# Summing the head outputs' squares where the outputs become final, and an output stage with batched factors, one mixing product, the norm's affine on VectorE and another order of pools

## The chip, the cores and the metric

One core of a Trainium2 chip runs the whole kernel. The metric is the device time of one execution in microseconds (us). The engines are named as in the profile: PE is TensorE (matrix multiplications and transposes; PEld its weight loads), DVE is VectorE, ACT is ScalarE, POOL is GpSimd, SP is SyncE, which issues all transfers between the memory (HBM) and the on-chip memory (SBUF). Matrix products accumulate in PSUM.

## The reference

A trunk of two layers runs over 2048 latent tokens with 256 context tokens in front, model width 1024. All is float32. In each layer the stream is normalised and modulated, projected, and split among three branches: a bidirectional gated delta scan (4 heads of 128 outputs, here A), a neighbourhood attention (4 heads of 64, B) and a bidirectional gated linear attention (4 heads of 64, C, "GLA"). A and C are sums of a forward and a backward pass, and each head of them is divided by its root mean square. Then all are gated, joined and projected, and the result is added to the stream and normalised again:

```
def head_rmsnorm_gate(o, w, z):
    o = o * lax.rsqrt(jnp.mean(o * o, -1, keepdims=True) + 1e-6) * w
    return o.reshape(b_, l, h * dv) * jax.nn.silu(z)
...
    y = concatenate([head_rmsnorm_gate(oa, gdn_norm[i], a_z), ob * silu(b_z),
                     head_rmsnorm_gate(oc, gla_norm[i], c_z)]) @ w_out[i]
    x = layer_norm(DN_ALPHA * x + gate * y) * ln_g[i] + ln_b[i]
```

Layer 0 gives 18 tiles of 128 tokens (2 context, 16 latent), layer 1 the 16 latent ones.

## The kernel before

Each layer of the kernel is a sequence of stages. Every large product is made of three float32 matmuls per 128 rows of depth (high by high, low by high, high by low; `dense_mm`, L185 to L190), so a value that goes into one is first split into a high part (written by ScalarE) and the rest (by VectorE).

The branches leave their outputs in memory. GLA (`Gla.chunk`, `Gla.reverse`) writes its forward output to OC; the reversal reads it back, adds its own part (L558) and stores it again. The delta scan (`Gdn.step`, L978 to L1041) goes forward and backward at once, two heads at a time. A step multiplies on TensorE (pk, pv), scales the result on ScalarE (v, L1013), multiplies again (pd) and updates the state on VectorE; v is on the chain from one step to the next. The direction that reaches a chunk second loads the first one's output from OA (L1035), adds its own (L1036) and stores the sum (L1040). Attention (`Natten.pair`) runs interleaved with the scan.

The output stage is class `Out`. `weights` loads w_out (raw), scales and splits it (wh on ScalarE, L1297; wl on VectorE, L1298). `run` has two parts for each tile. `mixed(n)` loads oa, ob, oc and the gates g, squares and sums each head of oa and oc on ScalarE (L1337, L1338; each writes a sum that a second short instruction reads out), makes the factor r of each head on VectorE with a square root on ScalarE (L1341 to L1346), multiplies outputs, factors and gates on VectorE (4 of 128 columns, L1350; 4 of 64, L1351; one of 256, L1352), transposes the product on TensorE (L1358) and splits it (mh on ScalarE, L1360; ml on VectorE, L1361). `finish(n)` makes the 48 matmuls of the tile into two PSUM tiles py, gates each (L1373), adds the stream x (L1374), takes the statistics, and normalises:

```
            b = P.tile([128, 1], F32, tag="pnb", name="pnb")
            nc.vector.scalar_tensor_tensor(b, mu, -1.0, r, op0=ALU.mult, op1=ALU.mult)
            eng = nc.vector if n == len(tiles) - 1 else nc.gpsimd
...
                nc.scalar.activation(y[:, s], y[:, s], AF.Identity, bias=b, scale=r)
                eng.tensor_tensor(y[:, s], y[:, s], self.g[:, 0, s], op=ALU.mult)
                eng.tensor_tensor(y[:, s], y[:, s], self.g[:, 1, s], op=ALU.add)
```

In layer 0 it also makes the next layer's normalised, modulated and transposed input M from y (`after`, with TensorE's L153 and ScalarE's L135).

The order of instructions on each engine is not written by hand: a scheduler lays the program's instructions out by its own time model, and buffers are taken from pools (a name, a number of buffers, a side of SBUF). A pool opened over memory that earlier tiles still use makes its first writers wait for those tiles. Instructions of one engine run in that order; a wait holds up what is queued behind it.

Of the kernel before, what the change touches and what calls it, by code (L numbers as in the profile page):

```python
# [160 lines left out]
def stage_p1(e, P, ps, xsrc, modT, M):  # L161

    for b in range(NB):
# [8 lines left out]
        for t in range(TPB):  # L172
            modulate(e, P, ps, xs[t], mu[:, t:t + 1], r[:, t:t + 1], b * TPB + t, modT, M)

# [153 lines left out]
class Gla:  # L328
# [180 lines left out]
    def chunk(self, c, i, A, E, et, V):  # L509
        e, nc, P, ps = self.e, self.e.nc, self.p, self.ps  # L510
        t0 = i * 128
        if c >= self.first:
# [10 lines left out]
            nc.sync.dma_start(self.OC[c], o1)  # L523

# [15 lines left out]
    def reverse(self):  # L540
        e, nc, P, ps = self.e, self.e.nc, self.p, self.ps
        for n, c in enumerate([1, 0] + list(range(NT - 1, 1, -1))):
# [17 lines left out]
            nc.sync.dma_start(self.OC[c], o1)  # L560

# [14 lines left out]
class Gdn:  # L576
# [4 lines left out]
    def __init__(self, e, ctx, conv_w, a_log, dt_bias, first):  # L581
# [19 lines left out]
        self.nW = c.tile(sh, F32, name="nW")  # L601
        self.conv_w = conv_w
# [375 lines left out]
    def step(self, s, d, c, n):  # L978
# [55 lines left out]
        if c in s.seen:  # L1034
            nc.sync.dma_start(ot, self.OA[c, :, h0:h0 + 2])  # L1035
            nc.vector.tensor_tensor(ot, ot, po, op=ALU.add)  # L1036
        else:
            s.seen.add(c)
            nc.scalar.copy(ot, po)
# [226 lines left out]
class Out:  # L1266
# [14 lines left out]
    def __init__(self, e, ctx):  # L1281
# [3 lines left out]
        self.P, W1, self.P1, W2 = (pool(n, b, "right") for n, b in (("op", 2), ("ow", 1), ("oi", 2), ("ox", 1)))  # L1285
# [25 lines left out]

    def load(self, P, n, w, src):
# [4 lines left out]
    def run(self, pss, tiles, G2, OA, na, OC, nq, xsrc, xdst, after):  # L1317

        e, nc = self.e, self.e.nc

        def mixed(n):
            t, P, ps = tiles[n], self.P1, pss[n % 2]
            ld = lambda n, w, src: self.load(P, n, w, src)
            oa = ld("oa", 512, OA[t].rearrange("p h d -> p (h d)"))
            ob = P.tile([128, 256], F32, tag="ob", name="ob")
            if t < 2:
                nc.sync.dma_start(ob, na.OBc[t])
            else:
                for i in range(4):
                    o = 64 * (t % 2) + 32 * (i // 2)  # L1330
                    nc.sync.dma_start(ob[32 * i:32 * i + 32], na.OB[t // 2 - 1, i % 2, o:o + 32])
            oc = ld("oc", 256, OC[t])
            g2 = ld("g2", 1024, G2[t])
            ms = P.tile([128, 8], F32, tag="ms", name="ms")
            sq = P.tile([128, 128], F32, tag="sq", name="sq")
            for h in range(4):
                nc.scalar.activation(sq, oa[:, h * 128:(h + 1) * 128], AF.Square, accum_out=ms[:, h:h + 1])  # L1337
                nc.scalar.activation(sq[:, :64], oc[:, h * 64:(h + 1) * 64], AF.Square, accum_out=ms[:, 4 + h:5 + h])  # L1338
            n_ = nq[:, :, t]
            f = P.tile([128, 8], F32, tag="f", name="f")  # L1340
            nc.vector.scalar_tensor_tensor(f[:, 0:4], n_, 1.0 / 128, n_, op0=ALU.mult, op1=ALU.mult)  # L1341
            nc.vector.memset(f[:, 4:8], 1.0 / 64)
# [194 lines left out]
```

## Time and profile before

| | |
|---|---|
| median of 3 runs | 4004.79 us (3985.05 to 4007.02) |
| profiled execution | 3995.01 us |
| its span | 3992.9 us |
| busy in the span: PE, PEld | 3626.0 us (91%), 3113.1 us (78%) |
| busy in the span: DVE, ACT, POOL | 2521.8 us (63%), 1660.0 us (42%), 810.2 us (20%) |
| mean granted PE clock | 0.913 of full speed |

The trace is of one execution. The span runs from its first to its last recorded instruction. Busy times of different engines overlap, and the shares are means over stages that differ.

### The profile page before, as it was taken

The page shows a single profiled execution, that of the slowest core. Times are in us where ns is not written, and L with a number is a line of the kernel's source. Part 1 is how long each engine was busy: PE and PEld are TensorE (multiplying, and loading weights), DVE is VectorE, ACT ScalarE, POOL GpSimd, SP SyncE. Part 2 cuts the span into 40 slices and gives each one's busy share as a digit, 9 for nine tenths or more (in the row PEclk, how much of TensorE's full clock was granted, in tenths as well). Part 3 has the DMA queues.
Part 4 walks back from the last instruction along what each step waited for, and adds up shares of the span by engine and source line. Part 5 has one row for each costly group of instructions (what it writes and reads, how often), then busy time and mean ns, then how long its engine had stood idle before and what let it go on. Part 6 is the DMA issues. An engine that isn't in the chain of part 4 may idle for free.

```text
span 3992.9 us, 77074 instructions
## 1 busy us (share of the span) xinstructions
PE 3626.0 (91%) x27262; PEld 3113.1 (78%) x27262; DVE 2521.8 (63%) x7471; ACT 1660.0 (42%) x4387; POOL 810.2 (20%) x1182
## 2 busy tenths in 40 slices
PE   7999998899989999897898999999999898989788
PEld 3777787579977888896676778887998788879676
DVE  5465462668975676356875556527798766753587
ACT  4533231335433454446545333213454244545342
POOL 0121111210101332221232211112111132331133
PEclk8988988899999998898898888899999998988899
DMA  9843435876687876666647443268776887775753
GB/s 312 280 147 105 133 112 169 245 232 201 205 276 219 246 229 189 187 196 214 203 132 232 152 147 115 100 210 251 215 232 201 285 228 205 228 217 150 219 160 111
DMA packets 756088, 787.57 MB, mean 197 GB/s; under 512 B 190207, under 2 KB 665207, under 8 KB 755703
## 3 DMA queue, kind: packets, MB, share of 16 engines
q1 hardware_dynamic: 755702, 782.64, 63.6%
q8 instruction: 216, 3.54, 0.4%
q14 instruction: 170, 1.38, 0.1%
HBM read 548.41 MB, written 234.03 MB: 196 GB/s over the span
## 4 chain that ended last, share of the span: by engine, by line
PE 55%; DMA 19%; DVE 16%; ACT 4%; issue 3%; SPq 2%; POOL 0%; DVEq 0%; ACTq 0%; POOLq 0%
PE p L190 29%; DMA mm<-MS 3%; PE p L1245 3%; DMA gb<-GR 2%; PE p L104 2%; DMA kk<-KK 2%; DMA raw<-in_w_in 1%; PE py L190 1%; PE po L1030 1%; PE pk L999 1%; PE pv L1010 1%; DMA oa<-OA 1%; PE pd L1017 1%; PE pt L1236 1%; DVE y L1374 1%
## 5 line engine op out<-in xcount | busy, mean ns | idle before, releaser
L190 PE MATMUL p<-mm,wh 128*128 128x384 f32 (+1 forms) x3648 | 1004.0, 354 | 67.2 <-DMA mm<-MS 21.4
L190 PEld LDWEIGHTS p<-mm,wh 128*128 128x128 f32 (+1 forms) x3648 | 667.8, 192 | 133.7 <-DMA mm<-MS 36.9
L190 PE MATMUL p<-mm,wl 128*128 128x384 f32 (+1 forms) x1824 | 635.1, 350 | 1.8 <-DVE wl L182 1.8
L190 PE MATMUL p<-wh,mm 128*128 128x512 f32 (+1 forms) x1696 | 570.5, 409 | 14.5 <-DMA mm<-MS 4.9
L190 PEld LDWEIGHTS p<-wh,mm 128*128 128x128 f32 x1696 | 329.1, 197 | 92.0 <-DMA mm<-MS 8.4
L649 DVE SCALAR_TENSOR_TENSOR acc<-pre,cw,acc 128x384 f32<-128x384 f32 (+1 forms) x576 | 351.8, 629 | 39.2 <-ACT acc L647 35.8
L190 PEld LDWEIGHTS p<-mm,wl 128*128 128x128 f32 (+1 forms) x1824 | 348.9, 191 | 22.8 <-issue 14.6
L190 PE MATMUL p<-wl,mm 128*128 128x512 f32 (+1 forms) x848 | 341.5, 403 | 4.3 <-DVE wl L182 4.3
L190 PE MATMUL py<-wh,mh 128*128 128x512 f32 x544 | 221.7, 410 | 17.1 <-ACT mh L1360 13.2
L190 PE MATMUL py<-wh,ml 128*128 128x512 f32 x544 | 213.9, 405 | 8.7 <-DVE ml L1361 8.7
L190 PE MATMUL py<-wl,mh 128*128 128x512 f32 x544 | 217.8, 402 | 0.0
L190 PEld LDWEIGHTS p<-wl,mm 128*128 128x128 f32 x848 | 166.5, 196 | 38.5 <-DVE wl L182 4.8
L992 POOL TENSOR_TENSOR kd<-kk,eD 128x256 f32<-128x256 f32 x144 | 90.4, 628 | 476.4 <-DMA kk<-KK 225.6
L1224 ACT ACTIVATE w<-w,mn 128x696 f32<-128x696 f32 (+2 forms) x136 | 112.9, 830 | 143.9 <-DVE mn L1221 142.6
L1383 POOL TENSOR_TENSOR y<-y,g 128x1024 f32<-128x1024 f32 x32 | 77.5, 2423 | 416.0 <-ACT y L1382 416.0
L639 POOL COPY pre<-pre 128x4 f32<-128x4 f32 x120 | 75.0, 627 | 416.4 <-DVE acc L649 244.1
L913 DVE TENSOR_TENSOR tmp<-M 96x30 f32<-96x30 f32 (+4 forms) x360 | 127.1, 353 | 27.7 <-issue 11.3
L1245 PE MATMUL p<-v,wl 120*128 120x64 f32 (+1 forms) x960 | 141.1, 286 | 0.0
L853 DVE SCALAR_TENSOR_TENSOR gb<-gb,Gt,mats 128x128 f32<-128x128 f32 x288 | 86.7, 358 | 83.0 <-DMA gb<-GR 82.8
L1261 DVE SCALAR_TENSOR_TENSOR zt<-zt,p 128x256 f32<-128x256 f32 (+1 forms) x102 | 51.4, 506 | 138.8 <-ACT zt L1260 131.9
L190 PEld LDWEIGHTS py<-wh,mh 128*128 128x128 f32 x544 | 106.4, 196 | 41.4 <-ACT mh L1360 16.1
L914 DVE TENSOR_TENSOR M<-M,tmp 96x30 f32<-96x30 f32 (+4 forms) x360 | 130.4, 362 | 6.1
(307 smaller groups left out, 8021.8 us busy)
## 6 DMA issues: line engine op xcount, KB each, us to landing
mm<-MS SPq DMA_DIRECT2D x384, 384.0 KB
kk<-KK SPq DMA_DIRECT2D x144, 512.0 KB
MS<-mm SPq DMA_DIRECT2D x96, 384.0 KB
raw<-in_w_in SPq DMA_DIRECT2D x104, 256.0 KB
w<-in_w_mod SPq DMA_DIRECT2D x96, 256.0 KB
M<-m SPq DMA_DIRECT2D x36, 512.0 KB
mm<-M SPq DMA_DIRECT2D x96, 192.0 KB
KK<-kq SPq DMA_DIRECT2D x96, 192.0 KB
```

The costliest lines, as they stand in the source:

```text
L104: nc.tensor.matmul(p, e.cc[:, k + j], w[:, j], start=k + j == 0, stop=k + j == KD - 1)
L190: e.nc.tensor.matmul(p, x(k), y(k), start=n == 0, stop=n == 3 * KD - 1)
L639: nc.gpsimd.tensor_copy(pre[:, 0:4], pre[:, m:m + 4])
L649: nc.vector.scalar_tensor_tensor(acc[:, :n], pre[:, k:k + n], w(kind, k), acc[:, :n], op0=ALU.mult, op1=ALU.add)
L853: nc.vector.scalar_tensor_tensor(E[:, d, h], gb[:, d, h], self.G[:, d, c, h0 + h:h0 + h + 1], e.mats[:, 1 + d], op0=ALU.subtract, op1=ALU.min)
L913: nc.vector.tensor_tensor(tv, col, row, op=ALU.mult)
L914: nc.vector.tensor_tensor(o, o, tv, op=ALU.add)
L992: nc.gpsimd.tensor_tensor(kd, kv[:, :, 0], self.eD[:, d, c, h0:h0 + 2].unsqueeze(2).to_broadcast([128, 2, 128]), op=ALU.mult)
L1224: nc.scalar.activation(w[:, a, 0:256 + nk], w[:, a, 0:256 + nk], AF.Exp, bias=m[:, a:a + 1], scale=-1.0, accum_out=sm[:, a:a + 1])
L1245: nc.tensor.matmul(p[:, a], l, r, start=j == 0, stop=j == len(parts) - 1)
L1261: nc.vector.scalar_tensor_tensor(th[:, :n], th[:, :n], 1.0, z, op0=ALU.add, op1=ALU.mult)
L1383: eng.tensor_tensor(y[:, s], y[:, s], self.g[:, 0, s], op=ALU.mult)
```

## The change

The squares leave the output stage. A new function `squares` makes them on ScalarE where a head's output becomes final: after GLA's second chunk and each of its reversal's additions, and after each addition of the scan. Their sums stay in a small tile `ms` in SBUF, for all 18 tiles. `factors` makes the factors of many tiles at once on VectorE, without a square root on ScalarE: for the first two tiles, and then for the others. In `mixed` the three outputs go into one tile of 1024 columns; ScalarE scales each head in place, and one VectorE product with the gates makes the mix. In `finish` the normalisation and its affine are two VectorE instructions, for all tiles. The mixing of tile n+1 is now issued ahead of finishing tile n, and the pools open in another order, with a pool `om` for mix, mh, ml and y.

```
+def squares(e, P, x, w, c, i):
+
+    for h in range(x.shape[1] // w):
+        jk = P.tile([128, w], F32, tag="sq", name="sq", bufs=1)
+        e.nc.scalar.activation(jk, x[:, h * w:(h + 1) * w], AF.Square, accum_out=e.ms[:, c, i + h:i + h + 1])
...
             nc.sync.dma_start(self.OC[c], o1)
+            if c == 1:
+                squares(e, P, o1, 64, c, 4)
...
             nc.vector.tensor_tensor(o1, o1, pO, op=ALU.add)
             nc.vector.scalar_tensor_tensor(S, S, self.etr[:, c:c + 1], self.dSr[:, c], op0=ALU.mult, op1=ALU.add)
             nc.sync.dma_start(self.OC[c], o1)
+            squares(e, P, o1, 64, c, 4)
...
+        e.ms = c.tile([128, NT, 8], F32, name="ms")
...
             nc.vector.tensor_tensor(ot, ot, po, op=ALU.add)
+            squares(e, P, ot.rearrange("p h t -> p (h t)"), 128, c, h0)
...
-        self.P, W1, self.P1, W2 = (pool(n, b, "right") for n, b in (("op", 2), ("ow", 1), ("oi", 2), ("ox", 1)))
+        self.PM, W1, self.P1, self.P, W2 = (pool(n, b, "right") for n, b in (("om", 2), ("ow", 1), ("oi", 2), ("op", 2), ("ox", 1)))
...
+    def factors(self, nq, t0, t1, tag):
+
+        e, nc, P = self.e, self.e.nc, self.P1
+        q = nq[:, :, t0:t1].rearrange("p h t -> p t h")
+        ms = e.ms[:, t0:t1]
+        v = P.tile([128, t1 - t0, 8], F32, tag=tag, name="v", bufs=1)
+        nc.vector.tensor_tensor(v[:, :, 0:4], q, q, op=ALU.mult)
+        nc.vector.scalar_tensor_tensor(v[:, :, 0:4], v[:, :, 0:4], 1.0 / 128, ms[:, :, 0:4], op0=ALU.mult, op1=ALU.mult)
+        nc.vector.tensor_scalar(v[:, :, 4:8], ms[:, :, 4:8], 1.0 / 64, None, op0=ALU.mult)
+        nc.vector.tensor_scalar(v, v, 1e-6, None, op0=ALU.add)
+        r = rsqrt_(e, P, v, [128, t1 - t0, 8], tag)
+        nc.vector.tensor_tensor(r[:, :, 0:4], r[:, :, 0:4], q, op=ALU.mult)
+        return r
...
+        lo = min(tiles)
+        rs = [self.factors(nq, tiles[0], tiles[0] + 2, "fa"), None]
+
         def mixed(n):
             t, P, ps = tiles[n], self.P1, pss[n % 2]
-            ld = lambda n, w, src: self.load(P, n, w, src)
-            oa = ld("oa", 512, OA[t].rearrange("p h d -> p (h d)"))
-            ob = P.tile([128, 256], F32, tag="ob", name="ob")
+            if n == 2:
+                rs[1] = self.factors(nq, lo, NT, "fb")
+            r = rs[0][:, n] if n < 2 else rs[1][:, t - lo]
+            o = P.tile([128, D], F32, tag="o", name="o")
+            nc.sync.dma_start(o[:, 0:512], OA[t].rearrange("p h d -> p (h d)"))
             if t < 2:
-                nc.sync.dma_start(ob, na.OBc[t])
+                nc.sync.dma_start(o[:, 512:768], na.OBc[t])
             else:
                 for i in range(4):
-                    o = 64 * (t % 2) + 32 * (i // 2)
-                    nc.sync.dma_start(ob[32 * i:32 * i + 32], na.OB[t // 2 - 1, i % 2, o:o + 32])
-            oc = ld("oc", 256, OC[t])
-            g2 = ld("g2", 1024, G2[t])
-            ms = P.tile([128, 8], F32, tag="ms", name="ms")
-            sq = P.tile([128, 128], F32, tag="sq", name="sq")
-            for h in range(4):
-                nc.scalar.activation(sq, oa[:, h * 128:(h + 1) * 128], AF.Square, accum_out=ms[:, h:h + 1])
-                nc.scalar.activation(sq[:, :64], oc[:, h * 64:(h + 1) * 64], AF.Square, accum_out=ms[:, 4 + h:5 + h])
-            n_ = nq[:, :, t]
-            f = P.tile([128, 8], F32, tag="f", name="f")
-            nc.vector.scalar_tensor_tensor(f[:, 0:4], n_, 1.0 / 128, n_, op0=ALU.mult, op1=ALU.mult)
-            nc.vector.memset(f[:, 4:8], 1.0 / 64)
-            nc.vector.tensor_tensor(ms, ms, f, op=ALU.mult)
-            nc.vector.tensor_scalar(ms, ms, 1e-6, None, op0=ALU.add)
-            r = rsqrt_act(e, P, ms, [128, 8], "or")
-            nc.vector.tensor_tensor(r[:, 0:4], r[:, 0:4], n_, op=ALU.mult)
-            mix = g2 if n < 2 else self.P.tile([128, D], F32, tag="mix", name="mix")
-            for h in range(4):
-                s, u, v = slice(h * 128, h * 128 + 128), slice(h * 64, h * 64 + 64), slice(768 + h * 64, 832 + h * 64)
-                nc.vector.scalar_tensor_tensor(mix[:, s], oa[:, s], r[:, h:h + 1], g2[:, s], op0=ALU.mult, op1=ALU.mult)
-                nc.vector.scalar_tensor_tensor(mix[:, v], oc[:, u], r[:, 4 + h:5 + h], g2[:, v], op0=ALU.mult, op1=ALU.mult)
-            nc.vector.tensor_tensor(mix[:, 512:768], ob, g2[:, 512:768], op=ALU.mult)
+                    k = 64 * (t % 2) + 32 * (i // 2)
+                    nc.sync.dma_start(o[32 * i:32 * i + 32, 512:768], na.OB[t // 2 - 1, i % 2, k:k + 32])
+            nc.sync.dma_start(o[:, 768:1024], OC[t])
+            g2 = self.load(P, "g2", 1024, G2[t])
+            for h in range(8):
+                s = slice(128 * h, 128 * h + 128) if h < 4 else slice(512 + 64 * h, 576 + 64 * h)
+                nc.scalar.activation(o[:, s], o[:, s], AF.Copy, scale=r[:, h:h + 1])
+            P = self.PM
+            mix = g2 if n < 2 else P.tile([128, D], F32, tag="mix", name="mix")
+            nc.vector.tensor_tensor(mix, o, g2, op=ALU.mult)
             mh = P.tile([128, KD, 128], F32R, tag="mh", name="mh")
             ml = P.tile([128, KD, 128], F32R, tag="ml", name="ml")
             for q in range(2):
@@ -1365,7 +1383,7 @@
             t, P, ps = tiles[n], self.P, pss[n % 2]
             gate = self.gt[1 if t < 2 else 0]
             x = self.load(P, "x", 1024, xsrc(t))
-            y = P.tile([128, D], F32, tag="y", name="y")
+            y = self.PM.tile([128, D], F32, tag="y", name="y")
             for q in range(2):
                 p = ps.tile([128, 512], F32, tag="py", name="py", bufs=2)
                 s = slice(512 * q, 512 * q + 512)
@@ -1373,15 +1391,11 @@
                 nc.vector.tensor_tensor(y[:, s], p, gate[:, s], op=ALU.mult)
                 nc.vector.scalar_tensor_tensor(y[:, s], x[:, s], ALPHA, y[:, s], op0=ALU.mult, op1=ALU.add)
             mu, r = ln_stats(e, P, [y], 1, "pn", rsqrt_act)
-            b = P.tile([128, 1], F32, tag="pnb", name="pnb")
-            nc.vector.scalar_tensor_tensor(b, mu, -1.0, r, op0=ALU.mult, op1=ALU.mult)
-            eng = nc.vector if n == len(tiles) - 1 else nc.gpsimd
             parts = 2 if n == len(tiles) - 1 else 1
             for q in range(parts):
                 s = slice(D // parts * q, D // parts * (q + 1))
-                nc.scalar.activation(y[:, s], y[:, s], AF.Identity, bias=b, scale=r)
-                eng.tensor_tensor(y[:, s], y[:, s], self.g[:, 0, s], op=ALU.mult)
-                eng.tensor_tensor(y[:, s], y[:, s], self.g[:, 1, s], op=ALU.add)
+                nc.vector.scalar_tensor_tensor(y[:, s], y[:, s], mu, self.g[:, 0, s], op0=ALU.subtract, op1=ALU.mult)
+                nc.vector.scalar_tensor_tensor(y[:, s], y[:, s], r, self.g[:, 1, s], op0=ALU.mult, op1=ALU.add)
             nc.sync.dma_start(xdst(t), y)
             if after:
                 after(t, y, x)
@@ -1391,8 +1405,8 @@
             m.append(mixed(n))
             yield
         for n in range(len(tiles)):
-            if n > 1:
-                m.append(mixed(n))
+            if 1 < n + 1 < len(tiles):
+                m.append(mixed(n + 1))
             finish(n, *m[n])
 
 
```

What the scheduler makes of it stands in the order of instructions. On VectorE, in the middle of layer 1's output stage, before (L1351, L1352: the mix; L1343 to L69 with ora: the factors; L1373, L1374: the output):

```order
L1350 SCALAR_TENSOR_TENSOR mix<-oa,ory,g_43064 128x128
L1351 SCALAR_TENSOR_TENSOR mix<-oc,ory,g_43064 128x64
L1352 TENSOR_TENSOR mix<-ob,g_43064 128x256
L1361 TENSOR_TENSOR ml<-pt,mh 128x512
L1343 TENSOR_TENSOR ms<-ms,f 128x8
L1344 TENSOR_SCALAR ms<-ms 128x8
L1341 SCALAR_TENSOR_TENSOR f<-nq 128x4
L1342 MEMSET f 128x4
L1373 TENSOR_TENSOR y<-py,gt 128x512
L69 RECIPROCAL ora<-ms 128x8
L1374 SCALAR_TENSOR_TENSOR y<-x,y 128x512
```

The same place now, from the second ml of one tile to the mix of the next (L1379 was L1361, L1391 was L1373, L1392 was L1374):

```order
L1379 TENSOR_TENSOR ml<-pt,mh 128x512
L122 BN_STATS pnst<-y 128x6
L123 BN_AGGR pnmv<-pnst 128x2
L125 TENSOR_SCALAR pnv<-pnmv 128x1
L1397 SCALAR_TENSOR_TENSOR y<-y,pnmv,g 128x1024
L69 RECIPROCAL pna<-pnv 128x1
L71 TENSOR_TENSOR pna<-pny 128x1
L72 SCALAR_TENSOR_TENSOR pna<-pna,pnv 128x1
L73 SCALAR_TENSOR_TENSOR pny<-pna,pny 128x1
L1398 SCALAR_TENSOR_TENSOR y<-y,pny,g 128x1024
L1391 TENSOR_TENSOR y<-py,gt 128x512
L1370 TENSOR_TENSOR mix<-o,g_43236 128x1024
```

The small operations of the factors are gone, the nine of the mix are one (L1370), and the two affine steps (L1397, L1398) stand between the statistics and the next tile's sum.

On ScalarE, the end of layer 1's scan, before (L1013: v of the scan; L1238, L1239, L1230: the attention; L1297: w_out):

```order
L1238 COPY wl<-pt 120x256
L1239 COPY wl<-pt 80x128
L1230 COPY wc<-pt 128x512
L1238 COPY wl<-pt 120x256
L1239 COPY wl<-pt 80x128
L1013 ACTIVATE v<-pv,Wt 128x128 x16
L1297 ACTIVATE wh_41510<-raw,cwo 128x512
L1297 ACTIVATE wh_41617<-raw,cwo 128x512
```

And now (L1024 is the former L1013, L180 the squares, L1250 and L1251 the attention, L1309 w_out):

```order
L1250 COPY wl<-pt 120x256
L1251 COPY wl<-pt 80x128
L180 ACTIVATE sq,ms<-o 128x128 x4
L1024 ACTIVATE v<-pv,Wt 128x128 x4
L180 ACTIVATE sq,ms<-o 128x128 x4
L1024 ACTIVATE v<-pv,Wt 128x128 x4
L180 ACTIVATE sq,ms<-o 128x128 x4
L1309 ACTIVATE wh_41587<-raw,cwo 128x512
L1309 ACTIVATE wh_41669<-raw,cwo 128x512
```

The 16 activations of the last steps ran without anything between; now four squares (one for each head and direction) stand between the groups of v.

On SP's queue of transfers, the end of layer 0's scan, before (L1040: a sum of the scan is stored; L1250: attention; L1309, L1310: ln_g, ln_b):

```order
L1040 DMA OA<-o 128x256
L1250 DMA OB<-po 128x128
L1309 DMA g<-in_ln_g 128x1024
L1310 DMA g<-in_ln_b 128x1024
L1314 DMA x<-in_ctx 128x1024 x2
L1314 DMA oa<-OA 128x512
L1327 DMA ob<-OBc 128x256
```

And now (L1052 and L1262 are the former L1040 and L1250):

```order
L1052 DMA OA<-o 128x256
L1306 DMA raw<-in_w_out 128x512 x2
L1052 DMA OA<-o 128x256
L1262 DMA OB<-po 128x128
L1356 DMA o<-OA 128x512
L1358 DMA o<-OBc 128x256
L1363 DMA o<-OC 128x256
L1340 DMA g_20121<-G_100 128x1024
```

The first tile's outputs and the first weights stood behind ln_g, ln_b and two tiles of the stream; now ln_g, ln_b and the stream stand later.

## Rows read from the trace of the kernel before

**Rows 1.** Windows (output stages 0, 1; scan 0): us, busy PE, PEld, DVE, ACT, POOL.

```profile
1816.40:2097.40 281.00, 246.96 (x1116) 200.23 (x1116) 223.79 (x700) 157.09 (x508) 77.67 (x35) 0.93 0.53 169
3766.00:3978.10 212.10, 195.25 (x884) 157.51 (x885) 176.88 (x502) 84.77 (x309) 71.69 (x29) 0.98 0.47 152
1290.00:1795.00 505.00, 464.62 (x4348) 431.44 (x4347) 286.19 (x929) 246.52 (x679) 138.84 (x282) 0.92 0.73 210
```

**Rows 2.** Timeline, end of layer 0's output stage: start, us, engine, operation.

```profile
2060.34 1.29 DVE L1373 TENSOR_TENSOR y<-py,gt 128x512 f32<-128x512 f32 x2 [1.24 <-ACT x L135]
...
2085.42 1.09 PE L153 MATMUL p<-ident,x 128*128 128x128 f32 x8
...
2097.92 1.29 DVE L1373 TENSOR_TENSOR y<-py,gt 128x512 f32<-128x512 f32 x2 [1.23 <-ACT x L135]
```

**Rows 3.** Waits of PE, layer 0's then layer 1's output stage: us, times, longest.

```profile
PE pt L1358 <- DVE ml L1361: 9.8, 5, 4.5
PE p L153 <- ACT x L135: 7.3, 6, 2.6
PE py L190 <- DVE ml L1361: 5.3, 2, 4.4
PE py L190 <- DVE y L1373: 3.9, 3, 2.7
...
PE py L190 <- ACT mh L1360: 9.4, 9, 2.7
PE pt L1358 <- DVE ml L1361: 4.7, 5, 1.0
PE py L190 <- DVE ml L1361: 3.4, 1, 3.4
```

**Rows 4.** Timeline of DVE and POOL in layer 1's output stage.

```profile
3864.43 0.28 DVE L1351 SCALAR_TENSOR_TENSOR mix<-oc,ory,g 128x64 f32<-128x64 f32 x1
3864.63 0.34 DVE L1350 SCALAR_TENSOR_TENSOR mix<-oa,ory,g 128x128 f32<-128x128 f32 x1
3864.76 2.48 POOL L1383 TENSOR_TENSOR y<-y,g 128x1024 f32<-128x1024 f32 x1 [6.12 <-ACT y L1382]
3864.89 2.43 DVE L1351 SCALAR_TENSOR_TENSOR mix<-oc,ory,g 128x64 f32<-128x64 f32 x1
```

**Rows 5.** DVE's groups in layer 1's output stage: busy us, mean ns.

```profile
L1374 DVE SCALAR_TENSOR_TENSOR y<-x,y 128x512 f32<-128x512 f32 x32 | 31.9, 999 | 0.4
L1350 DVE SCALAR_TENSOR_TENSOR mix<-oa,ory,g 128x128 f32<-128x128 f32 x56 | 28.4, 524 | 7.8 <-PE pt L1358 7.8
L1351 DVE SCALAR_TENSOR_TENSOR mix<-oc,ory,g 128x64 f32<-128x64 f32 x56 | 27.9, 509 | 0.0
L1352 DVE TENSOR_TENSOR mix<-ob,g 128x256 f32<-128x256 f32 x14 | 5.8, 413 | 0.0
...
L1341 DVE SCALAR_TENSOR_TENSOR f<-nq 128x4 f32<-128x4 f32 x16 | 2.4, 157 | 0.0
```

**Rows 6.** ACT's groups in layer 1's output stage.

```profile
L1337 ACT ACTIVATE sq<-oa 128x128 f32<-128x128 f32 x64 | 19.8, 309 | 38.6 <-DMA oa<-OA 35.8 <-DVE y L1373 1.2
...
L1337 ACT ACTIVATION_READ_ACCUMULATOR sq<-oa 128x1 f32 x64 | 11.9, 187 | 0.0
```

**Rows 7.** Timeline of PE at the start of layer 0's output stage.

```profile
1813.32 1.26 PE L1358 MATMUL pt<-ident,g 128*128 128x128 f32 x4 [19.23 <-DVE g L1350]
```

**Rows 8.** The line L1013 (v of the scan), whole span: ACT's idle time before it.

```profile
  PE pv L1010: 108.6, 69
```

**Rows 9.** The line L1036 (the scan's additions): DVE's idle time before it.

```profile
  DMA o<-OA: 34.8, 21
```

**Rows 10.** Timeline of DVE at the end of the span.

```profile
3978.75 2.39 DVE L1374 SCALAR_TENSOR_TENSOR y<-x,y 128x512 f32<-128x512 f32 x1
...
3982.49 0.69 DVE L1374 SCALAR_TENSOR_TENSOR y<-x,y 128x512 f32<-128x512 f32 x1
...
3986.55 1.40 DVE L1383 TENSOR_TENSOR y<-y,g 128x512 f32<-128x512 f32 x2 [0.93 <-ACT y L1382]
```

## The prediction

> **What bounds the kernel now.** The page's first part gives TensorE 3626 of 3992.9 us and VectorE 2522. That is an average over stages, so I read the windows view of the stages that the change touches [rows 1]. In the layer-0 output stage TensorE is busy 247 of 281 us and VectorE 224; in that of layer 1 195 of 212.1 and 177. Neither is full, so I looked for what TensorE would need alone. Late in layer 0 the mixes are long done; TensorE then runs without a gap, and the first and the last of four consecutive tiles' first gated sums are 2060.34 and 2097.92, so 37.58/3 = 12.53 us a tile [rows 2]. A layer-1 tile has no M transposes, whose row has 1.09 us with its end lying over the next matmul; I take off 0.85: 11.7 us. So layer 0 needs 18 x 12.53 = 226 us and takes 281, an excess of 55; layer 1 needs 16 x 11.7 = 187 and takes 212, an excess of 25.
>
> Who keeps TensorE waiting there? The waits view [rows 3] names VectorE's ml and y and ScalarE's mh and x: 9.8 + 7.3 + 5.3 + 3.9 = 26.3 us in layer 0, 9.4 + 4.7 + 3.4 = 17.5 in layer 1. These are all late because VectorE is late, and the timeline shows why [rows 4]: a 64-wide mix takes 0.28 us, and 2.43 when it starts just after GpSimd's 2.48 us multiply by g, ending with it. Over the layer-1 stage L1374 averages 999 ns, where one outside GpSimd's stretches takes 0.69; L1350 averages 524 and L1351 509 against 340 and 280 [rows 4, 5, 10]. 32 x 0.31 + 56 x 0.18 + 56 x 0.23 = 33 us of VectorE's 177 are this waiting; layer 0, with 17 GpSimd tiles for 15, has some 37.
>
> The Trainium skill, "SBUF — State Buffer", section "Who interferes with whom", says that a VectorE instruction with two SBUF inputs contends with a GpSimd instruction that reads SBUF, and that whichever issues first blocks the other for its whole length. The row of 2.43 us agrees. By the rule alone both GpSimd operations of a tile could cost VectorE their full length, 4.9 us a tile; the means above give 2.1, since part of VectorE's work in those stretches reads PSUM.
>
> **The change, part by part.**
>
> *Affine to VectorE, GpSimd free.* Removed per tile: two GpSimd operations, a 1024-wide ScalarE pass, the small pnb. Added: two 1024-wide VectorE operations. The trace has 256 elements at 413 ns [rows 5] and 512 at 690 [rows 10]; the slope, 1.08 ns, gives 1.24 us for 1024. Bounds: 1.0 (if there is a fixed part that the slope hides) and 2.4 (GpSimd's own time for it). I take 1.24, the same engine's.
>
> *Mix.* Nine operations (4 x .34 + 4 x .28 + .41 unstalled, less some overlap at their ends, about 2.2 us) become one 1024-wide, 1.24 us at most. The scaling goes to eight ScalarE copies, about 1.8 us at the length of a square [rows 6], in the place of eight squares with their reads, 4 x (.31 + .19) and somewhat less for the narrow ones, some 3.3. ScalarE thus falls by 1.5 + 1.24 us a tile.
>
> *Factors.* Some ten operations of about 0.16 us [rows 5] leave each tile; 28 in all come back per layer at the stage's head (about 4 us there, under the first weights' conversion).
>
> VectorE in layer 1, per tile: 177/16 = 11.05, less 2.1 (stalls), 1.6 (factors), 1.0 (mix), plus 2.5 (affine): 8.9, against TensorE's 11.7. Layer 0: 224/18 = 12.4, by the same steps 10.2, against 12.53. With two affine operations at the 2.4 us bound it would be 12.5: then it is level with TensorE.
>
> *Order.* The mixing product of a tile is put one tile ahead, so its transposes stand in the previous tile's matmuls; the order of VectorE shows the two affine steps between a tile's statistics and the next tile's first gated sum, then the mix. What is late next is the first tile's weights and loads, so I don't give the whole excess back: of layer 0's 55 I take the 26 that the waits name, of layer 1's 25 I take 13 (the 17.5 without a quarter for the mh of the first two tiles, which the weights delay too). Bounds: nothing, if those waits are replaced by others, and 55 + 25.
>
> *Start of the stage.* TensorE idles 19.23 us between the scan and the first transpose in layer 0 [rows 7]; the loads of o are now ahead of gt, ln_g, ln_b and two x on SP's queue, eight squares, a table load and a chain of small operations leave the path, eight copies and one product come. I take 7 in layer 0, and 2 in layer 1, where weights hold the next matmuls. Bounds 0 and 12 each.
>
> *Tail.* The last tile loses pnb and a ScalarE pass that VectorE waited 0.93 us for, and its first L1374 took 2.39 us in place of 0.69 because GpSimd held it [rows 10]. 0.2 + 0.9 + 1.7 = 2.8, so 3 us.
>
> *Squares that move.* All 136 squares of 128 columns go to the scan, two behind each of 68 adds, at (.31 + .19) less overlap = .43 us: 58 us of ScalarE over both layers; the 64-wide ones, some 50 us, go behind GLA's chunks and reversals. Nothing in the trace shows ScalarE there with them. In the layer-0 scan ScalarE is busy 246.5 of 505 us and TensorE 465 [rows 1]; the activation behind which the chain hangs, v, finds ScalarE waiting for pv 69 times, 108.6 us in all [rows 8], so there is a mean slack of 1.6 us at each of those. But a square waits for its add, the add for a load of OA (34.8 us in 21 cases [rows 9]), and ScalarE's queue behind it waits too: v of the next step, and the attention's softmax. The cover is the attention's matmuls; the last two or three steps of a scan have none left. Bounds: 0, and 58 + 35 = 93. I take 8, near the lower end, because 3 x 2 uncovered steps of 4 squares (1.74 us) in the two layers' last scans make 10, some of it slack. The GLA squares lie beside dense matmuls and off any chain: 2 (bounds 0 and 50).
>
> **Sum**, against the profiled execution (span 3992.9, time 3995.0): -26 - 13 - 7 - 2 - 3 + 8 + 2 = -41, so 3954. That execution lies 10 us under the median of the three runs (4004.8), inside their spread of 22; the median of the changed kernel may lie above its profiled one in the same way, so I add 4: **3958**.
>
> **Rivals.**
>
> 1. *VectorE becomes the bound in layer 0.* If a 1024-wide affine costs nearer 2.4 us, or x comes late and the round's fixed order makes VectorE's mix wait behind it, the 26 us stay: 3995 - 15 = 3980. For it: VectorE is already at 80% there. Against: the layer-1 figure of 8.9.
> 2. *The stall was slack.* If the excess is weights, x loads and M's transposes, and TensorE's waits only change their name, starts and tail bring 12 and squares cost 10: 3993.
> 3. *Slower: the squares sit on the scan's chain.* Each of the 34 places where both directions add gets four squares ahead of the next v; if all 58 us and the OA waits (35) are seen, -51 + 93 gives 4037. It decides from 51 of 93, that is 1.5 us for each of the 34 places. For it: in the last steps nothing else stands between. Against: TensorE has 8% idle in the scan stage, and ScalarE is half idle.
>
> **How the numbers follow.** Forecast 0.69, rival 1 0.13, rival 2 0.10, rival 3 0.08. Own range of the forecast 3930 to 3978, from 70 gained (most of the excess, with starts) to 20. With rivals 1 and 2 taken in: 3922 to 3994, which leaves out rival 3 and a tail below. A measurement here can tell about 0.5% from no change (20 us, to 3985): faster 0.80 (forecast and most of rival 1), same 0.12, slower 0.08.
>
> **What would show it.** GpSimd empty in both output stages; no VectorE operation there above 1.4 us; L1397 and L1398 near 1.24 us; tiles 12.5 and 11.7 us apart; TensorE's waits for ml and mh nearly gone; first py 7 us sooner after the last OB store in layer 0. The scan windows should grow by less than 5 us each; if v waits or TensorE's wait for v grows by tens of us, rival 3 holds. The forecast is wrong if the tile pitch stays near 13 in layer 1 with GpSimd empty.

## The result, and the profile after

The changed kernel takes 3959.6 us (median of 4 runs, 3951.5 to 3967.0), the kernel before 3997.8 beside it; the ratio is 0.9913, 95% interval 0.989 to 0.9937. That is 0.87% faster, and the forecast was 3958. The sum was right; several of its terms were not, and their errors cancel: it put the gain in the output stages too low, and had too little or nothing for two losses, in layer 0's scan and on the way into layer 1. (The profiles of two experiments, old_pools and no_ahead, are of slow executions, with a granted clock of 0.83 to 0.86 in every scan; their scans are not read, and the first was run again.)

The profiled execution of the changed kernel has a span of 3965.2 us, 27.7 under that of the kernel before. Cut at the same events in both traces:

| stretch | before | after | difference |
|---|---|---|---|
| up to the first scan step of layer 0 (pv) | 1286.6 | 1280.6 | -6.0 |
| layer 0's scan, first pv to last po | 506.6 | 526.7 | +20.1 |
| to the first output matmul (py) | 23.3 | 18.5 | -4.8 |
| layer 0's output matmuls | 280.6 | 240.2 | -40.4 |
| to layer 1's first gate (zt) | 44.0 | 66.8 | +22.8 |
| to layer 1's scan | 1090.4 | 1091.7 | +1.3 |
| layer 1's scan | 513.1 | 511.8 | -1.3 |
| to its first output matmul | 22.2 | 25.3 | +3.1 |
| layer 1's output matmuls | 213.0 | 192.9 | -20.1 |
| tail | 13.1 | 10.7 | -2.4 |

The windows of the changed kernel, in the order and with the columns of [rows 1], and behind them layer 1's scan (in brackets the number of instructions; the last three figures of a row are the mean granted clock, the busy share of the DMA engines and GB/s):

```profile
1825.80:2066.00 240.20, 231.58 (x1112) 189.81 (x1112) 194.51 (x436) 129.70 (x345) 5.40 (x6) 0.99 0.64 208
3761.60:3954.50 192.90, 192.56 (x888) 157.55 (x888) 148.57 (x263) 53.34 (x161) 0.00 (x0) 0.99 0.49 166
1280.60:1807.30 526.70, 485.95 (x4415) 449.80 (x4414) 288.59 (x925) 276.43 (x828) 141.34 (x290) 0.88 0.71 203
3224.50:3736.30 511.80, 471.44 (x4318) 437.91 (x4316) 291.86 (x938) 263.66 (x782) 140.64 (x287) 0.88 0.72 208
```

TensorE is now full in layer 1's output stage (192.56 of 192.9 us) and nearly so in layer 0's; GpSimd is all but empty in both. In layer 0 the same matmuls also keep TensorE busy for less time, 231.6 us in place of 247.0, at a granted clock of 0.99 in place of 0.93. VectorE's groups in layer 1's output stage, beside [rows 5]:

```profile
L1392 DVE SCALAR_TENSOR_TENSOR y<-x,y 128x512 f32<-128x512 f32 x32 | 22.0, 687 | 0.5
...
L1398 DVE SCALAR_TENSOR_TENSOR y<-y,pny,g 128x1024 f32<-128x1024 f32 x15 | 19.3, 1284 | 0.5
L1397 DVE SCALAR_TENSOR_TENSOR y<-y,pnmv,g 128x1024 f32<-128x1024 f32 x15 | 19.1, 1275 | 0.0
L1370 DVE TENSOR_TENSOR mix<-o,g 128x1024 f32<-128x1024 f32 x14 | 17.0, 1217 | 3.1 <-DMA g<-G 3.1
```

The stream's addition is back at 687 ns (999 before), and the 1024-wide operations cost 1.22 to 1.28 us, as the slope said. TensorE's waits in the two stages, beside [rows 3] (layer 0's first, with the 34 us after its last output matmul):

```profile
PE p L153 <- ACT x L135: 22.1, 7, 10.3
PE pt L1376 <- DVE ml L1379: 3.6, 1, 3.6
...
PE py L197 <- ACT mh L1378: 1.8, 1, 1.8
PE py L197 <- DVE ml L1379: 0.3, 1, 0.3
```

The waits for mh and ml are nearly gone, 17.5 to 2.1 us in layer 1. One is left: the transposes of M wait for x. Only 3.9 of its 22.1 us lie before the last output matmul (7.3 in the kernel before); 18.2 come behind it. The timeline at the end of layer 0 shows where (TensorE, then SP's queue):

```profile
2087.38 1.97 PE L153 MATMUL p<-ident,x 128*128 128x128 f32 x8 [10.30 <-ACT x L135]
2093.63 1.97 PE L153 MATMUL p<-ident,x 128*128 128x128 f32 x8 [4.28 <-ACT x L135]
...
2097.71 0.53 SPq L158 DMA_DIRECT2D M<-m  x1
2098.28 1.88 SPq L227 DMA_DIRECT2D raw<-in_w_in  x2
```

The last output matmul starts at 2066.0; the last tiles' normalisation and transposes go on to 2095.6, with TensorE idle for 18.2 us of that, and the first weights of the next layer are asked for at 2098.28, behind the last store of M. The same queue in the kernel before:

```profile
2097.25 0.93 SPq L220 DMA_DIRECT2D raw<-in_w_in  x2
...
2154.41 0.51 SPq L158 DMA_DIRECT2D M<-m  x1
```

There the last output matmul started at 2097.1, the weights were asked for at once, and the last four tiles' M followed up to 2154, under the next layer's matmuls. That overlap is lost, so more than half of the 40 us that TensorE won in layer 0 is waited away.

### The profile page after: what moved, and what is told of

It is laid out like the page before. It is cut to its first block, busy times and chain, and to the rows that moved or that the text cites. A ratio compares the mean times of both kernels' runs of the same rounds, so it can differ in the third digit from the quotient of the medians.

```text
span 3965.2 us, 76683 instructions
## 1 busy us (share of the span) xinstructions
PE 3615.5 (91%) x27262; PEld 3108.7 (78%) x27262; DVE 2467.1 (62%) x6983; ACT 1689.4 (43%) x4587; POOL 654.5 (17%) x1118
## 5 line engine op out<-in xcount | busy, mean ns | idle before, releaser
L197 PEld LDWEIGHTS p<-mm,wl 128*128 128x128 f32 (+1 forms) x1824 | 347.0, 190 | 22.2 <-issue 16.0
L1257 PEld LDWEIGHTS p<-v,wl 120*128 120x128 f32 (+1 forms) x960 | 132.2, 207 | 0.7
L1233 DVE CUSTOM_DVE_ANT_0 w<-pl,tb,mn 128x440 f32<-128x440 f32 (+1 forms) x128 | 81.9, 640 | 79.5 <-PE pl L1192 68.0
L1041 PE MATMUL po<-v,A 128*128 128x128 f32 x544 | 116.0, 299 | 15.3 <-DVE S L1033 12.0
```

Of the source, the lines that this page charges most:

```text
L197: e.nc.tensor.matmul(p, x(k), y(k), start=n == 0, stop=n == 3 * KD - 1)
L1041: nc.tensor.matmul(po[:, h], A[:, h], v[:, h], start=True, stop=not n)
L1233: nc.vector.tensor_tensor_reduce(w[:, a, 256:256 + nk], pl, bias[:, a], scale=1.0, scalar=mn[:, 0, a:a + 1], op0=ALU.add, op1=ALU.min, acc ...
L1257: nc.tensor.matmul(p[:, a], l, r, start=j == 0, stop=j == len(parts) - 1)
```

## The experiments

All ratios are against the kernel before, run on the same chip beside the experiment; (after) is the changed kernel, 0.9913.

**gps_affine**: the changed kernel, the affine back on GpSimd.

```
+            b = -mu * r;  eng = nc.vector if last tile else nc.gpsimd
-                nc.vector.scalar_tensor_tensor(y, y, mu, g0, subtract, mult)
-                nc.vector.scalar_tensor_tensor(y, y, r, g1, mult, add)
+                nc.scalar.activation(y, y, AF.Identity, bias=b, scale=r)
+                eng.tensor_tensor(y, y, g0, mult);  eng.tensor_tensor(y, y, g1, add)
```

> The changed kernel with the affine of the norm on GpSimd again (and the ScalarE pass and the small pnb with it). If GpSimd's hold on VectorE is what the change removed: two-input VectorE operations of 2.4 us are back, the span of the output matmuls in layer 1 goes from 193 us to 205 or more, in layer 0 from 240 to 260 or more, and the time is 15 to 35 us above the changed kernel's. If the gain is from the single mix, the factors and the tile put ahead: both spans stay within 5 us, and the time within 10.

Ratio 0.9990 (0.9956 to 1.0024): the whole gain is gone, some 31 us, as expected. Layer 0's output matmuls take 257.9 us, just under the 260 expected, and layer 1's 196.9, well under the 205. VectorE's groups in layer 1's stage, and GpSimd's:

```profile
L1392 DVE SCALAR_TENSOR_TENSOR y<-x,y 128x512 f32<-128x512 f32 x32 | 36.0, 1124 | 1.0
L1370 DVE TENSOR_TENSOR mix<-o,g 128x1024 f32<-128x1024 f32 x14 | 28.1, 2004 | 5.0 <-DMA g<-G 4.5 <-DMA x<-X 0.2 <-issue 0.2
L1391 DVE TENSOR_TENSOR y<-py,gt 128x512 f32<-128x512 f32 x32 | 22.0, 687 | 17.2 <-PE py L197 13.9 <-DMA out<-y 3.3
...
L1401 POOL TENSOR_TENSOR y<-y,g 128x1024 f32<-128x1024 f32 x15 | 41.4, 2759 | 147.8 <-ACT y L1400 147.8
```

The instructions with two inputs in SBUF, L1392 and L1370, go from 687 and 1217 ns to 1124 and 2004 with the affine beside them on GpSimd; L1391, which reads one of its inputs from PSUM, keeps its 687 (683 in the changed kernel). The hold is shown. In layer 1 the rest of the change absorbs most of it: the output matmuls grow by 4 us there, where the whole change had taken 20 off. Which part absorbs it isn't shown.

**dve_affine_only**: the kernel before with only that part of the change.

```
-            eng = nc.vector if n == len(tiles) - 1 else nc.gpsimd
-  ScalarE normalise, eng.tensor_tensor * g, + b
+  two VectorE scalar_tensor_tensor, (y - mu) * g and y * r + b
```

> The kernel before with only the affine moved to VectorE. If GpSimd's hold was the cost: the layer-1 output matmuls go from 213 us to about 200, layer 0's from 281 to about 260, the scan keeps its length, and the time is 20 to 35 us under the kernel before, so near the changed kernel's. If the gain is from the rest of the change: less than 10 us under the kernel before.

Ratio 0.9917 (0.9884 to 0.9949): all of the change's gain from a few lines. Its output matmuls, of layer 0 and layer 1, by the tile py (first and last start):

```profile
L190 PE MATMUL py<-wh,mh x288: 387/389/796, 1811.6 to 2068.1; 128*128 128x512 f32 x144
...
L190 PE MATMUL py<-wh,mh x256: 387/389/793, 3737.7 to 3935.5; 128*128 128x512 f32 x128
```

257 and 198 us, against 281 and 213; the scan keeps its 507.9. So the rest of the change, from here to (after), shortens the matmuls by 17 and 5 us and gives it back elsewhere.

**no_scan_sq** and **no_sq**: where do layer 0's 20 us come from?

```
-            squares(e, P, ot.rearrange("p h t -> p (h t)"), 128, c, h0)     # no_scan_sq, no_sq
-                squares(e, P, o1, 64, c, 4)                                 # no_sq: GLA's two calls as well
+        e.nc.vector.memset(e.ms, 1.0)
```

> The changed kernel without the scan's squares (their sums are set to 1, so the A factors are not those of the reference). If the squares on ScalarE made layer 0's scan longer (507 us before, 527 in the changed kernel, first pv to last po): it falls back to about 507, layer 1's stays at 512, and the time is some 15 to 20 us under the changed kernel's. If the squares are hidden and the 20 us are another layout of the schedule: the scan stays within 5 us of 527 and the time within 8.

> The changed kernel with all squares left out, the scan's and GLA's (the sums are set to 1, so the factors are not those of the reference). TensorE's order in layer 0's scan is then row for row that of the kernel before; with either kind of squares in it is another. If the 20 us that layer 0's scan lost came with that other order: the scan (first pv to last po) is 507 us, within 4, in place of 527. If they came from something else in the change (pools, the tile put ahead): 527 stays.

Without the scan's squares the ratio is 0.991 (0.9877 to 0.9943), no change. The scan stays long, as no_scan_sq's rows of its first product (pv, first and last start) and its last (po) show:

```profile
L1022 PE MATMUL pv<-R,X x272: 270/275/582, 1276.5 to 1796.8; 128*128 128x128 f32 x136
...
L1044 PE MATMUL po<-S,kk x272: 274/275/580, 1282.0 to 1802.8; 128*128 128x128 f32 x136
```

526.3 us with not one square in the scan, so it can be as long without ScalarE's time for them. Without any squares it is 503.0, ratio 0.9837 (0.9808 to 0.9866). What goes with the length is the order of TensorE's rows in the scan. Seven profiles with the former order (before, dve_affine_only, no_sq, dve_x3, before_x3, sq_out, sq_out_x4) have 496 to 512.5 us; four with the changed kernel's order (after, gps_affine, x3, old_pools_again) have 526.6 to 529.1; no_scan_sq has a third order. The last row of a table of the kernel before, over its scan from 1286.6 to 1793.2:

```profile
sum 506.60, PE 467.12 PEld 433.73 DVE 285.94 ACT 248.77 POOL 138.84; mean PE 93.42 PEld 86.75 DVE 57.19 ACT 49.75 POOL 27.77
```

TensorE is idle for 39.5 us of it, and for 40.8 of the changed kernel's 526.7 (its third window above). So the 20 us are not waits, for squares or for anything else: TensorE is busy 486 us in place of 467 for nearly the same work, at a mean granted clock of 0.88 in place of 0.92. In the traces' clock records 126 us of the scan stand at the lower of the two levels (1.2 and 2.4 GHz), against 85 before; an estimate: 41 us more at half speed are worth some 20. Windows of 20 us near the start of the scan, of the kernel before and then of the changed one (whose scan begins 6 us sooner):

```profile
1300.00:1320.00 20.00, 15.75 (x99) 13.61 (x97) 8.85 (x29) 3.64 (x11) 8.87 (x23) 0.91 1.02 251
1320.00:1340.00 20.00, 15.66 (x116) 13.98 (x116) 13.09 (x42) 9.92 (x28) 6.81 (x12) 0.83 0.95 283
1340.00:1360.00 20.00, 19.96 (x279) 18.33 (x278) 11.24 (x40) 15.68 (x46) 7.07 (x15) 1.00 0.87 241
1360.00:1380.00 20.00, 18.87 (x192) 16.98 (x191) 11.78 (x40) 9.21 (x25) 4.19 (x9) 0.83 0.85 267
```

```profile
1300.00:1320.00 20.00, 12.05 (x62) 10.25 (x60) 6.38 (x21) 2.32 (x7) 9.27 (x24) 0.83 0.94 234
1320.00:1340.00 20.00, 14.01 (x112) 12.41 (x112) 14.82 (x47) 8.94 (x26) 6.34 (x11) 0.83 0.92 268
1340.00:1360.00 20.00, 17.95 (x165) 15.95 (x165) 11.37 (x36) 9.18 (x27) 4.37 (x9) 0.67 0.82 229
1360.00:1380.00 20.00, 20.00 (x162) 17.80 (x161) 2.99 (x10) 8.92 (x25) 2.68 (x7) 0.50 0.28 82
```

In the changed kernel TensorE idles 8 and 6 us in two stretches (it waits 10.9 us for the states S), and the granted clock then falls to 0.67 and 0.50, which is the lower level, 1.2 GHz, for the whole of a stretch in which TensorE never stops. It looks as if the gaps had cost the clock, but the same windows in old_pools_again, which has the same order of TensorE's rows in this scan, say otherwise:

```profile
1300.00:1320.00 20.00, 12.34 (x63) 10.65 (x62) 7.10 (x23) 2.32 (x7) 8.89 (x23) 0.83 0.90 229
1320.00:1340.00 20.00, 14.61 (x106) 12.89 (x106) 14.42 (x47) 8.28 (x23) 5.88 (x10) 0.82 0.87 264
1340.00:1360.00 20.00, 18.64 (x241) 16.46 (x240) 13.16 (x41) 14.66 (x43) 6.94 (x14) 1.00 0.88 243
1360.00:1380.00 20.00, 20.00 (x249) 18.46 (x248) 11.79 (x38) 11.36 (x33) 4.87 (x10) 1.00 0.72 234
```

There the gaps of the first three stretches are nearly the same (7.7, 5.4 and 1.4 us, against 8.0, 6.0 and 2.1), and the clock is full in the third and fourth. That execution lost its clock later, and its scan has the same 0.88 and 529.1 us. So the length goes with the order and with the clock; by what the order lowers the clock stays open.

**x3** and **before_x3**: is the reuse of the stream tile's buffers what is left in layer 0?

```
-            x = self.load(P, "x", 1024, xsrc(t))
+            x = P.tile([128, 1024], F32, tag="x", name="x", bufs=3)
+            nc.sync.dma_start(x, xsrc(t))
```

> The changed kernel with three buffers for the stream tile x in place of two. In the changed kernel layer 0's output matmuls end 30 us before the last transposes of M, and VectorE waits 18.5 us for x. If the reuse of x's two buffers (load, add, norm, transposes, next load) is what the output stage of layer 0 is left bound by: VectorE's wait for x falls under 6 us, the lag from the last output matmul to the last transposes of M falls from 30 us to 15 or less, and the time by 8 to 20 us. If it is VectorE's own chain behind the matmuls: the lag stays over 22 and the time within 5.

> The kernel before with three buffers for x and the affine left on GpSimd. If GpSimd's hold is the first bound and x the second: layer 0's output matmuls stay over 265 us (281 before) and layer 1's at 213, within 5. If x was the bound in layer 0 from the start and GpSimd only looked like it: layer 0's matmuls fall to 255 or less here too.

x3, on the changed kernel: 0.9755 (0.9707 to 0.9802), the best of all. TensorE's waits in layer 0's output stage and behind it:

```profile
PE p L197 <- ACT wh L186: 7.9, 2, 7.1
PE p L153 <- ACT x L135: 6.0, 1, 6.0
```

The wait of M's transposes falls from 22.1 to 6.0, the time from the last output matmul to M's last activation from 31 us to 15, and layer 0's stage up to layer 1's first zt from 307.0 to 281.1: 26 us, of which 8 are in the pace of the output matmuls (232.2 for 240.2). VectorE no longer waits for x, and the lag is the 15 expected; the time fell far more than the 8 to 20 us expected, 63 by the ratios. Of the profile's 57 us, another 25 are in layer 1's scan, 486 us for 512, where nothing was edited. On the kernel before, three buffers do nothing: 0.999 (0.996 to 1.0019), matmuls 284 and 223.4 us (the second longer than the 213 expected, unexplained). The hold was the first bound, and in the changed kernel x is the second.

**dve_x3**: the kernel before with both edits.

> The kernel before with the affine on VectorE and three buffers for x; TensorE's order in both scans is row for row that of the kernel before. If GpSimd's hold and the reuse of x are the two things that bound the output stages: layer 0's stage, from the first output matmul to the next layer's first zt, is 20 us or more shorter than with the affine on VectorE alone (301 us), both scans keep their 507 and 513, and the time is 35 to 60 us under the kernel before. If most of what three buffers gave beside the change came from another order in layer 1's scan (486 in place of 512): no more than 10 us better than the affine alone.

Ratio 0.9862 (0.9836 to 0.9888), 55 us under the kernel before and some 22 under the affine alone. Layer 0's stage to layer 1's first zt is 290.5 us against 300.8: 10, not the 20 expected. In that stage the wait that grows in place of x is TensorE's for ScalarE's mh, from 6.0 us with the affine alone to 16.4. So neither expected case came. Layer 0's scan is 12 us shorter too, 496 for 508 in one and the same order: two executions of one order can differ by that much.

**old_pools** and **old_pools_again** (the same kernel):

```
-        self.PM, W1, self.P1, self.P, W2 = ("om", 2), ("ow", 1), ("oi", 2), ("op", 2), ("ox", 1)
+        self.P, W1, self.P1, W2 = ("op", 2), ("ow", 1), ("oi", 2), ("ox", 1);  self.PM = self.P
```

> The changed kernel with the former order of pools (mix, mh, ml and y in op again). TensorE's order in layer 0's scan stays the changed kernel's; in layer 1's scan it is row for row that of the kernel with three x buffers. If the 486 us of that scan go with the order of its instructions: 486 here too, within 5, and 527 in layer 0. If they go with the single execution: 505 or more. If the new order of pools made the start of the output stage sooner (18.5 us in layer 0 in place of 23.3): it is 22 or more here; else it stays.

> The changed kernel with the former order of pools, once more, for an undisturbed profile. TensorE's order in layer 1's scan is row for row that of the kernel with three x buffers, which took 486 us there, against 512 in the changed kernel's order. If a scan's length goes with the order of its instructions: 480 to 493. If the 486 was one execution's chance: 503 or more.

Ratios 0.9822 (0.9786 to 0.9858), better than with the new order of pools, and 0.9886 (0.9834 to 0.9937, two runs), which alone can't be told from it. The profile of the second shows where it is shorter. SP's queue near the end of layer 0's outputs, which end at 2081:

```profile
2072.92 0.52 SPq L158 DMA_DIRECT2D M<-m  x1
2073.49 1.83 SPq L227 DMA_DIRECT2D raw<-in_w_in  x2
```

The next layer's weights are asked for 8 us before the outputs end, not 32 us after; from the first output matmul to layer 1's first zt it takes 292.4 us in place of 307.0, although the matmuls alone take 252 in place of 240. The start is as with the new pools (18.7 us): they did not make it sooner. And layer 1's scan, whose order on TensorE is row for row that of x3, is short in both. The windows of that scan in x3, in old_pools_again, and in sq_out (the former order):

```profile
3193.60:3680.00 486.40, 453.43 (x4317) 416.53 (x4316) 289.85 (x940) 264.18 (x782) 138.46 (x283) 0.93 0.76 217
```

```profile
3213.40:3705.10 491.70, 456.39 (x4318) 421.33 (x4316) 292.55 (x940) 262.89 (x783) 138.47 (x283) 0.92 0.76 215
```

```profile
3212.60:3731.10 518.50, 468.77 (x4293) 434.23 (x4292) 289.00 (x935) 242.62 (x660) 138.46 (x281) 0.88 0.72 205
```

Four profiles of the former order (before, no_scan_sq, dve_x3, sq_out) have 503 to 518.5 us at layer 1, and two of the order that no_sq has there, 494.7 and 506.7: within one order, executions differ by up to 15 us. Between x3 and sq_out the 32 us are about half busy time, with a granted clock of 0.93 against 0.88, and half idle time, 33 against 50 us.

**sq_out** and **sq_out_x4**: the changed kernel with the squares in the output stage, then with four x buffers too.

```
-  squares(...) in GLA and scan, factors() for many tiles with rsqrt_
+            squares(e, P, o[:, 0:512], 128, t, 0);  squares(e, P, o[:, 768:1024], 64, t, 4)
+            r = self.factors(nq, t, t + 1, "or")[:, 0]          # with rsqrt_act: the square root on ScalarE again
```

> The changed kernel with the squares back in the output stage (on ScalarE, from the tile o; factors made for each tile), all else as changed; TensorE's order in both scans is then row for row that of the kernel before. If the squares' place costs the changed kernel the 20 us of layer 0's scan: that scan takes 500 to 512 us, layer 1's 505 to 513, the layer-1 output matmuls stay under 199 us, and the time is 15 to 30 us under the changed kernel's. If squares in the output stage were a cost worth moving: the output matmuls grow by more than 15 us together and the time is no better than the changed kernel's.

> The same with four buffers for x. TensorE's order in layer 0's scan is that of the kernel before, in layer 1's that of the kernel without any squares, which took 495 us there. Expected if the account adds up: layer 0's scan 500 to 512, from the first output matmul of layer 0 to the next layer's first zt 285 us or less (307 in the changed kernel, 281 with three buffers), layer 1's scan 490 to 500, and a time 85 to 115 us under the kernel before. If squares in the output stage hold ScalarE and VectorE up there: less than 60 under it.

sq_out: 0.9903 (0.9882 to 0.9924), the changed kernel's time. Layer 0's scan is back at 508.0 (19 less), the start takes 2.4 us more, the output matmuls 8 and 2.4 more, and layer 1's scan has 518.5 in this execution. My 15 to 30 us did not come. Moving the squares costs 19 us in layer 0's scan, by the order that came with it, and saves some 13 in the output stages; the 7 us more in layer 1's scan lie within what executions of that order differ by. sq_out_x4: 0.9765 (0.9737 to 0.9792), 94 us under the kernel before, within what the account gives, though layer 1's scan (506.7) and the stage of layer 0 (287.7) are longer than expected; it equals x3 within the intervals.

**no_ahead**: each tile's mixing in its own turn again.

```
-            if 1 < n + 1 < len(tiles):
-                m.append(mixed(n + 1))
+            if n > 1:
+                m.append(mixed(n))
```

> The changed kernel with each tile's mixing issued in its own turn again, as before, not one tile ahead. TensorE's order in layer 0's scan stays the changed kernel's (527 us). With the affine alone the output matmuls took 257 us in layer 0 and 198 in layer 1, with the whole change 240 and 193. If putting the mix a tile ahead made that difference: 250 or more and 197 or more here. If the single mix and the factors made it: within 5 us of 240 and 3 of 193.

Ratio 0.9976 (0.9946 to 1.0007). Without the tile ahead most of the gain is gone, some 25 us. Its only profile has output matmuls of 255.7 and 200.4 us, at a granted clock of 0.96 and 0.98 there, on the side expected if the tile ahead made the difference (250 or more, 197 or more). With one profile this is an indication; layer 1's scan has another order here too (that of gps_affine, 516 us).

## Why the prediction was right, and where its terms were not

**The mechanism** holds: GpSimd's affine stretched VectorE's two-input operations, and VectorE held up TensorE. dve_affine_only has the whole gain, gps_affine none, and the same instructions change length with GpSimd's work alone. Rival 2 (the stall was slack) falls. That "part of VectorE's work in those stretches reads PSUM", and so isn't held, is borne out by L1391 (683 ns without GpSimd's work, 687 with it).

**Output stages.** I took 26 us in layer 0 and 13 in layer 1 from the waits that the trace named; the matmul spans lost 40.4 and 20.1. As a measure of waits this was close: TensorE's idle time in the two windows fell from 34.0 to 8.6 us and from 16.9 to 0.3. The size was off because most of the rest is busy time, for which I had no term of its own: in layer 0 the matmuls took 15 us less at the higher clock (0.99 for 0.93). The excess of 55 held that, but I gave back only its waits. Layer 1 came near its floor (192.9 against 187, where I stopped at 199). In layer 0 the step that failed is "what is late next is the first tile's weights and loads". What is late next is the end of the stage: with TensorE ahead, the last three tiles still have to go through load of x, addition, norm and M, two buffers at a time, and the next layer's weights now stand behind them. That took 22.8 us back, so layer 0's stage with what follows won 17.6, not 26. x3 shortens that chain by 16 us, and with the former pools (old_pools_again) the weights come ahead of its end; each removes part of the loss. Rival 1 had named a late x as one way for VectorE to bind; it came true mostly at the end of the stage, and with 8 us in its pace (x3). VectorE's load itself was no bound: 10.8 and 9.3 us a tile by the windows, where I had 10.2 and 8.9.

**Starts and tail.** -4.8 and +3.1 against -7 and -2; tail -2.4 against -3. The new pools have no part in the first (old_pools_again: 18.7 us).

**Squares.** I put 8 us on the scans for ScalarE's time and its waits, and layer 0's scan lost 20, against the sign of under 5 that I gave. The bounds held it, the reason didn't: no_scan_sq has the same 526 us with no squares there, and TensorE's idle time in the scan grew by 1.3 us only. With squares anywhere ahead of the output stage, GLA's alone included, the scheduler's layout had another order in the scan, and all five profiles of those orders have a granted clock of 0.87 or 0.88 over it, against 0.91 or 0.92 in the seven of the former. Rival 3's chain of v and squares is not seen: TensorE's wait for v is 1.4 us over the whole of layer 0's scan. The 2 us for the GLA squares aren't seen either: the stretches with GLA changed by -6.0 and +1.3, and the first of them spreads over 1276.5 to 1287.4 us in the profiles with and without squares. That another order of the scan can cost or give 20 us with no instruction added there was in none of my cases.

**The sum**: -41 forecast, -28 between the two profiles, -38 between the medians. It was right partly because errors cancel: 22 us too little for the matmuls against 23 that I had not for the way into layer 1; what is left is mainly the scans, 11 us more than the 8 I gave them; the starts fell 7 us short, and the stretches ahead of the scans made that up. That the sum came within 2 us of the median is luck.

## What to carry to other kernels

Where one engine's work makes another's instructions longer, and the second holds up the bounding engine, move that work first: a few lines gave as much as the whole change. When the bounding engine gets faster, look at what leaves the stage last and at which loads wait behind it; a third buffer for the stream tile was worth 26 us there, and nothing in the kernel before. With a scheduler that lays out the whole program, compare the order in the stages that were not edited before putting a time down to the edit: kernels whose order differs can differ by 20 us in a stage that nobody edited, and even executions of one order differed by up to 16 us in a scan, so take more than one profile.

## What the runs showed of the hardware

VectorE's instructions with two inputs in SBUF got longer beside GpSimd's affine (128x512: 687 to 1124 ns on average, 128x1024: 1217 to 2004); one that reads PSUM and one tile in SBUF did not (683 and 687).

The length of layer 0's scan followed TensorE's granted clock and not its waits: idle 39.5 and 40.8 us, busy 467 and 486, at a mean clock of 0.92 and 0.88. In layer 1 it was both: busy 453 us and idle 33 at a clock of 0.93, busy 469 and idle 50 at 0.88. Short gaps alone don't tell where the clock falls: in two executions of one order, gaps of 8.0 and 6.0 us in two stretches of 20 were followed by a clock of 0.67 and 0.50, and gaps of 7.7 and 5.4 by 1.00 and 1.00. What decides it is not shown here.
